# Padding the split tiles so that successive buffers lie at other offsets modulo 256 bytes

## The chip, the core and the metric

The kernel runs on one core of a Trainium2 chip. The metric is the device time of one execution in microseconds (us). Three runs of the kernel before took 2083.59, 2081.73 and 2076.95 us: a median of 2081.73.

## What is computed

One layer of an encoder trunk, applied with the same weights to a prompt of 512 tokens and to a sample of 2048 tokens, 1024 wide. One projection of the normed input gives everything else:

```python
h = rms_norm(x, pre_g)
z = h @ w_in
(q, k, v, gate_a, u_b, gate_b, c_val, c_glu, gate_c,
 merge_a, merge_b, merge_c) = jnp.split(z, split_pts, axis=-1)
y_a = neighbourhood_attention(heads(q), heads(k), heads(v), rpb) * jax.nn.silu(gate_a)
y_b = fourier_mix(u_b) * jax.nn.silu(gate_b)
y_c = conformer_conv(c_val, c_glu, dw_w, dw_b, cn_g, cn_b) * jax.nn.silu(gate_c)
merged = (jax.nn.sigmoid(merge_a) * (y_a @ w_a)
          + jax.nn.sigmoid(merge_b) * (y_b @ w_b)
          + jax.nn.sigmoid(merge_c) * (y_c @ w_c))
return x + rms_norm(merged @ w_o, post_g)
```

The attention looks at a window of 8 rows by 16 columns on a grid 64 wide, with 8 heads of 64; the Fourier mix is the real part of a 2-D transform; the convolution has 31 taps.

## The kernel before

**Split operands.** Every large matmul works on fp32 numbers that are held as two parts, high and low, in one tile `[128, 2, n]` of type fp32r. `split` (L133) writes the high part with a copy on ScalarE (L136) and the low part with a subtraction on VectorE (L137). A product is then three matmuls with 128 contracted rows: high by high, high by low, low by high. In `narrow` (L170 to L184) they are L180 to L182, with the weights stationary and 512 tokens (256 in the merge) moving:

```python
nc.tensor.matmul(ps, lhsT=u[:, 0, s], rhs=r[:, 0], start=n == 0, stop=False)
nc.tensor.matmul(ps, lhsT=u[:, 0, s], rhs=r[:, 1], start=False, stop=False)
nc.tensor.matmul(ps, lhsT=u[:, 1, s], rhs=r[:, 0], start=False, stop=n == len(kts) - 1)
```

Each of them is a weight load of 128 columns (the rows of PEld) and a matmul (the rows of PE). A block is eight steps of the contraction (kt), so 24 matmuls into one PSUM bank. In `wide` (L186, L194 to L196) tokens are stationary and 256 columns of weights move.

**Stages.** The tokens come as five chunks of 512: chunk 0 is the prompt, 1 to 4 the sample. Chunks 1 and 2, then 3 and 4, then 0 are projected: `proj_c`, `proj_qk`, `proj_v`, `proj_u`, `gates` and `merge_gates` take one weight unit after another from a list (`stream`, L158), and `emit_unit` (L139) loads a unit and splits it into two `w` tiles of a pool with five buffers. The tokens of a chunk are eight tiles `hT`, made by `make_h` (L219) or `raw_h` (L233) in two rings of 8 and 10 buffers (`ring`, `ring2`). Attention, convolution and Fourier transform are generators that `pump` (L283) advances between steps of the projections, so that their small matmuls (scores L603 and L604, transposes L636, `pv` L647, channel mean L480) stand among the projection's on TensorE. All activations go out to HBM. At the end, for each half chunk of 256 tokens, `prepare` (L805) loads and gates the branches into `ysp` tiles, `merge` (L828) multiplies by the resident weights `wb` through `narrow` and makes `msp` tiles, and `finish` (L855) multiplies by the resident `wo` in L869 to L871, with `msp` stationary and 512 columns of `wo` moving. `resident` (L1060) makes `wb` and `wo`.

**What sets the order.** The program's own order and a scheduler set each engine's order before the run; DMAs go through SP's queue.

**Where the tiles lie.** A `w` or `hT` tile takes 2 x 512 x 4 = 4096 bytes of each partition, a `wb` or `wo` tile 8192, an `ysp` or `msp` tile 4096. All are multiples of 256, and so is the distance between high and low part and between column slices of 128. So all buffers of a pool, and every slice that a matmul takes of one, share one offset modulo 256. In the allocation that is 32 for `w` and `hT`, 224 for `ysp` and `wb`, 128 for `wo` and `msp`; for the attention's tiles and the channel mean's `sp` it is 96, for the channel mean's stationary `ones` 0. Of a moving operand and the weights beside it the two offsets are equal, but for the channel mean, the transposes, part of the scores, and at the borders between stages. The first 16 KB of each partition are set aside as DMA scratch.

Of the kernel before, what the change touches and what calls it, by code (L numbers as in the profile page):

```python
# [16 lines left out]
F32R = mybir.dt.float32r  # L17
# [7 lines left out]
P = 128  # L25
D = 1024
KT = 8
C = 512
# [74 lines left out]
    return out.astype(np.float32)  # L103


class Build:
    def __init__(self, tc, a, out_p, out_s):
        self.tc, self.nc, self.a = tc, tc.nc, a
        self.outs = (out_p, out_s)
# [29 lines left out]
    def emit_unit(self, src, pieces=1):  # L139

        raw = self.wraw.tile([P, 1024], F32, tag="wraw", name="wraw")
        n = 1024 // pieces
        for i in range(0, 1024, n):
            self.load = self.nc.sync.dma_start(raw[:, i: i + n], src[:, i: i + n])
        ws = []
        for i in range(2):
            w = self.wsp.tile([P, 2, 512], F32R, tag="w", name="w")
            self.low = self.split(w, raw[:, i * 512: i * 512 + 512])
            ws.append(w)
        return ws  # L150
# [68 lines left out]
    def make_h(self, c, pool, tiles, ring):  # L219

        nc = self.nc
        rrow = pool.tile([P, C], F32, tag="rrow", name="rrow", bufs=1)
        nc.sync.dma_start(rrow, self.rs[c].to_broadcast([P, C]))
        for kt in range(KT):
            xr = pool.tile([P, C], F32, tag="xr", name="xr", bufs=3)
            nc.sync.dma_start(xr, self.a["xT"][kt * P: kt * P + P, c * C: c * C + C])
            nc.vector.scalar_tensor_tensor(xr, xr, self.preg[:, kt:kt + 1], rrow, op0=ALU.mult, op1=ALU.mult)
            t = ring.tile([P, 2, C], F32R, tag="h", name="hT")
            self.split(t, xr)
            tiles.append(t)  # L230
            yield

    def raw_h(self, c, tiles, ring):  # L233

        nc = self.nc
        for i in range(4):
            xr = self.ap.tile([P, 2, C], F32, tag="psp" if i % 2 else "vsp", name="xr", bufs=2)
            src = self.a["xT"][2 * i * P: 2 * i * P + 2 * P, c * C: c * C + C].rearrange("(k p) t -> p k t", p=P)
            apart = c == 1 and i == 0
            if not apart:  # L240
                nc.sync.dma_start(xr, src)
            for k in range(2):
                if apart:
                    nc.sync.dma_start(xr[:, k], src[:, k])
                g = self.preg[:, 2 * i + k: 2 * i + k + 1]
                t = ring.tile([P, 2, C], F32R, tag="h", name="hT")
                nc.scalar.mul(t[:, 0], xr[:, k], g)
                nc.vector.scalar_tensor_tensor(t[:, 1], xr[:, k], g, t[:, 0].bitcast(F32),  # L248
                                               op0=ALU.mult, op1=ALU.subtract)
                tiles.append(t)  # L250
                yield
# [553 lines left out]
    def prepare(self, c, hh, pool):  # L805

        nc = self.nc
        tok = slice(hh * 256, hh * 256 + 256)
        ysp = {}
        for b2 in (2, 3, 0, 1):  # L810
            if b2 < 2:
                y, low = (pool.tile([P, 2, 256], F32, tag="yl", name="yl", bufs=3) for _ in range(2))
                for i, t in enumerate((y, low)):
                    nc.sync.dma_start(t, self.ya[c][2 * b2: 2 * b2 + 2, i, :, tok].rearrange("b p t -> p b t"))
                nc.gpsimd.tensor_tensor(y, y, low, op=ALU.add)
            else:
                y = pool.tile([P, 2, 256], F32, tag="yl", name="yl", bufs=3)
                nc.sync.dma_start(y, self.yd[c][2 * b2 - 4: 2 * b2 - 2, :, tok].rearrange("b p t -> p b t"))
            g = pool.tile([P, 2, 256], F32, tag="gl", name="gl", bufs=2)
            nc.sync.dma_start(g, self.sg[c][2 * b2: 2 * b2 + 2, :, tok].rearrange("b p t -> p b t"))  # L820
            nc.vector.scalar_tensor_tensor(y, y, 0.5 if b2 == 3 else 1.0, g, op0=ALU.mult, op1=ALU.mult)  # L821
            t = pool.tile([P, 2, 2, 256], F32R, tag="ysp", name="ysp", bufs=5)
            self.split(t, y)
            for i in range(2):
                ysp[2 * b2 + i] = t[:, :, i]
        return ysp

    def merge(self, c, hh, ysp, pool, thp):  # L828

        nc = self.nc  # L830
        tok = slice(hh * 256, hh * 256 + 256)
        msp = {}
        for m2 in range(4):
            acc = pool.tile([P, 2, 256], F32, tag="acc", name="acc", bufs=2)
            for i in range(2):
                m = 2 * m2 + i
                th = thp.tile([P, 3, 256], F32, tag="th", name="th", bufs=3)
                nc.sync.dma_start(th, self.th[c][m][:, :, tok])
                pb = self.mm()
                for x, kts in enumerate(((4, 5), (6, 7))):  # L840
                    self.narrow(pb[:, x * 256: x * 256 + 256], self.wb[m], lambda kt: ysp[kt], kts)
                pa = self.mm()
                self.narrow(pa[:, :256], self.wb[m], lambda kt: ysp[kt], (0, 1, 2, 3))
                nc.vector.scalar_tensor_tensor(th[:, 1:3], th[:, 1:3], 1.0, pb.rearrange("p (x t) -> p x t", x=2),  # L844
                                               op0=ALU.add, op1=ALU.mult)
                nc.vector.scalar_tensor_tensor(acc[:, i], th[:, 0], 1.0, pa[:, :256], op0=ALU.add, op1=ALU.mult)
                nc.gpsimd.tensor_tensor(th[:, 1], th[:, 1], th[:, 2], op=ALU.add)
                nc.vector.tensor_tensor(acc[:, i], acc[:, i], th[:, 1], op=ALU.add)
            t = pool.tile([P, 2, 2, 256], F32R, tag="msp", name="msp", bufs=5)
            self.split(t, acc)  # L850
            for i in range(2):
                msp[2 * m2 + i] = t[:, :, i]
        return msp
# [42 lines left out]
    def run(self):  # L896
        tc, nc, a = self.tc, self.nc, self.a
        with ExitStack() as ctx:
# [36 lines left out]
            ring = F(tc.tile_pool(name="ring", bufs=8, side="left"))  # L935
# [11 lines left out]
            hT = {c: [] for c in range(NCH)}  # L947
# [96 lines left out]
            def prefetch():  # L1044
                while self.pos < base + 135:
                    yield
                att.close()
                pa = E(tc.tile_pool(name="pa", bufs=1, side="right", reuse_waits="tile"))
                state["pa"] = pa
                while self.pos < base + 163:  # L1050
                    yield
                fft.close()
                state["y"] = self.prepare(1, 0, pa)
                wbp = E(tc.tile_pool(name="wbp", bufs=1, side="right", reuse_waits="tile"))
                self.wb = []
                for _ in resident(a["wb"], wbp, self.wraw, "wraw", "wb", self.wb):
                    for _ in range(4):
                        yield

            def resident(src, pool, raw, tag, nm, out):  # L1060
                for i in range(KT):
                    r = raw.tile([P, 1024], F32, tag=tag, name="wraw", bufs=3 if tag == "wraw" else 2)
                    nc.sync.dma_start(r, src[i])
                    w = pool.tile([P, 2, 1024], F32R, tag=f"{nm}{i}", name=nm)
                    self.split(w, r)
                    out.append(w)
                    yield
# [10 lines left out]
            for _ in resident(a["wo"], mp, mp, "x", "wo", self.wo):  # L1078
                pass
            pa, ysp = state["pa"], state["y"]  # L1080
            order = [(c, hh) for c in (1, 2, 3, 4, 0) for hh in range(2)]
            for n, (c, hh) in enumerate(order):
                msp = self.merge(c, hh, ysp, mp, pa)
                if n + 1 < len(order):
                    ysp = self.prepare(*order[n + 1], pa)
# [51 lines left out]


def program(arrays):
    nc = bacc.Bacc("TRN2", target_bir_lowering=False, num_devices=1)  # L1140
    a = {k: nc.dram_tensor(k, v.shape, mybir.dt.from_np(v.dtype), kind="ExternalInput").ap()
         for k, v in arrays.items()}
    out_p = nc.dram_tensor("y_prompt", (1, 512, D), F32, kind="ExternalOutput").ap()
    out_s = nc.dram_tensor("y_sample", (1, 2048, D), F32, kind="ExternalOutput").ap()
    with tile.TileContext(nc, schedule_with_timeline_sim=True) as tc:  # L1145
        Build(tc, a, out_p, out_s).run()
    return nc
# [8 lines left out]
```

## Time and profile before

| | before |
|---|---|
| median of 3 runs | 2081.73 us (2076.95 to 2083.59) |
| the profiled execution's own time | 2078.99 us |
| its span, first to last instruction | 2077.2 us |
| TensorE busy | 2050.4 us, 99% of the span, 11184 matmuls |
| weight loads (PEld) | 1773.8 us, 85% |
| VectorE, ScalarE, GpSimd busy | 62%, 39%, 15% |
| TensorE clock granted, mean over the span | 0.997 |
| HBM read and written | 284.47 and 109.58 MB, 190 GB/s |

The profile is of one execution. Line numbers are those of the kernel before. Matmuls are pipelined: a row's duration reaches past the start of the next matmul, so the pace is read from starts in the timeline, which gives them to 0.01 us; over many rows the rounding goes away. PE stands for TensorE's matmuls, PEld for its weight loads, DVE for VectorE, ACT for ScalarE, POOL for GpSimd, SP for the queue of DMAs.

### The profile page before, as it was taken

How to read it: one execution, taken by the hardware profiler on the slowest of the kernel's cores; microseconds unless marked ns; L12 is line 12 of the kernel's file. 1: busy time of each engine (PE TensorE's matmuls, PEld its weight loads, DVE VectorE, ACT ScalarE, POOL GpSimd, SP SyncE). 2: the span in 40 equal slices, each digit the busy share in tenths (PEclk: the TensorE clock that was granted, in tenths of full speed). 3: DMA queues.
4: the chain of work that ended last, by engine and by line, in shares of the span. 5: the costliest groups of instructions: out<-in, count | busy, mean ns of one | idle time of the engine just before them, and what ended most of it. 6: DMA issues, size and time to landing. Idle time of an engine off the chain costs nothing. (4 is left out here: it accounts for less than half of the span.)

```text
span 2077.2 us, 31264 instructions
## 1 busy us (share of the span) xinstructions
PE 2050.4 (99%) x11184; PEld 1773.8 (85%) x11184; DVE 1296.3 (62%) x2853; ACT 801.3 (39%) x1649; POOL 301.6 (15%) x318
## 2 busy tenths in 40 slices
PE   8899999999999999999999999999999999999998
PEld 6779888888888899888888888898888989999997
DVE  6374557565454546776666655898854666666655
ACT  6422234343332224555555555336654211111111
POOL 0000011111100002322222221003200122222211
PEclk9999999999999999999999999999999999999999
DMA  9694544444443545666566676779897755555532
GB/s 328 202 250 159 181 140 147 142 149 146 142 153 117 152 132 174 178 177 198 172 172 182 177 221 187 239 252 271 267 325 252 225 177 176 185 169 183 178 131 79
DMA packets 241195, 388.79 MB, mean 187 GB/s; under 512 B 25376, under 2 KB 137632, under 8 KB 239136
## 3 DMA queue, kind: packets, MB, share of 16 engines
q1 hardware_dynamic: 241040, 386.80, 60.1%
q8 instruction: 88, 1.44, 0.3%
q14 instruction: 67, 0.55, 0.1%
HBM read 284.47 MB, written 109.58 MB: 190 GB/s over the span
## 5 line engine op out<-in xcount | busy, mean ns | idle before, releaser
L180 PE MATMUL mm<-hT,w 128*128 128x512 f32 x1760 | 699.6, 398 | 15.0 <-ACT w L136 7.1
L181 PE MATMUL mm<-hT,w 128*128 128x512 f32 x1760 | 691.2, 393 | 0.0
L182 PE MATMUL mm<-hT,w 128*128 128x512 f32 x1760 | 690.7, 393 | 0.0
L180 PEld LDWEIGHTS mm<-hT,w 128*128 128x128 f32 x1760 | 332.1, 189 | 79.2 <-ACT w L136 7.3
L182 PEld LDWEIGHTS mm<-hT,w 128*128 128x128 f32 x1760 | 331.7, 188 | 70.3 <-DVE w L137 0.8
L181 PEld LDWEIGHTS mm<-hT,w 128*128 128x128 f32 x1760 | 332.4, 189 | 62.6 <-DVE hT L248 1.0
L137 DVE TENSOR_TENSOR w<-wraw,w 128x512 fp32r<-128x512 f32 x308 | 220.4, 719 | 142.7 <-ACT w L136 138.0
L136 ACT CAST w<-wraw 128x512 fp32r<-128x512 f32 x308 | 189.0, 618 | 201.8 <-PE mm L182 166.2
L459 DVE SCALAR_TENSOR_TENSOR acc<-cb,cw,acc 128x512 f32<-128x512 f32 (+1 forms) x300 | 237.3, 793 | 2.9
L180 PE MATMUL mm<-ysp,wb 128*128 128x256 f32 x640 | 181.7, 284 | 3.8 <-DVE nw_y L118 3.8
L182 PE MATMUL mm<-ysp,wb 128*128 128x256 f32 x640 | 181.7, 284 | 0.0
L181 PE MATMUL mm<-ysp,wb 128*128 128x256 f32 x640 | 181.7, 284 | 0.0
L611 ACT ACTIVATE p<-p,m 128x384 f32<-128x384 f32 (+2 forms) x160 | 102.3, 639 | 153.0 <-DVE m L610 127.8
L607 DVE CUSTOM_DVE_ANT_0 p<-s,bias 128x384 f32<-128x384 f32 (+2 forms) x160 | 92.6, 580 | 104.7 <-PE pt L636 88.1
L574 POOL TENSOR_TENSOR bias<-tab,mask 128x384 f32<-128x384 f32 x64 | 67.4, 1056 | 572.1 <-DVE m L607 529.4
L566 POOL TENSOR_TENSOR bias<-tab,mask 128x512 f32<-128x512 f32 x64 | 85.9, 1344 | 367.5 <-DVE m L607 353.7
L195 PE MATMUL mm<-w,hT 128*128 128x256 f32 x480 | 135.5, 283 | 0.0
L196 PE MATMUL mm<-w,hT 128*128 128x256 f32 x480 | 135.5, 283 | 0.0
L194 PE MATMUL mm<-w,hT 128*128 128x256 f32 x480 | 135.2, 284 | 0.0
L180 PEld LDWEIGHTS mm<-ysp,wb 128*128 128x128 f32 x640 | 123.2, 193 | 5.4 <-DVE th L844 4.0
L870 PE MATMUL po<-wo,msp 128*128 128x512 f32 x320 | 124.5, 390 | 0.0
L869 PE MATMUL po<-wo,msp 128*128 128x512 f32 x320 | 124.3, 391 | 0.1
(154 smaller groups left out, 3000.0 us busy)
## 6 DMA issues: line engine op xcount, KB each, us to landing
wraw<-wn SPq DMA_DIRECT2D x135, 512.0 KB
th<-z SPq DMA_DIRECT2D x120, 256.0 KB
th<-th SPq DMA_DIRECT2D x80, 384.0 KB
qsp<-qd SPq DMA_DIRECT2D x80, 256.0 KB
tab<-tab SPq DMA_DIRECT2D x40, 384.0 KB
w<-dftd SPq DMA_DIRECT2D x14, 1024.0 KB
vsp<-vds SPq DMA_DIRECT2D x256, 48.0 KB
qd<-zs SPq DMA_DIRECT2D x20, 512.0 KB
```

Of the source, the lines that this page charges most:

```text
L136: nc.scalar.copy(dst[:, 0], src)
L137: return nc.vector.tensor_tensor(dst[:, 1], src, dst[:, 0].bitcast(F32), op=ALU.subtract)
L180: nc.tensor.matmul(ps, lhsT=u[:, 0, s], rhs=r[:, 0], start=n == 0, stop=False)
L181: nc.tensor.matmul(ps, lhsT=u[:, 0, s], rhs=r[:, 1], start=False, stop=False)
L182: nc.tensor.matmul(ps, lhsT=u[:, 1, s], rhs=r[:, 0], start=False, stop=n == len(kts) - 1)
L194: nc.tensor.matmul(ps, lhsT=r[:, 0, q], rhs=w[:, 0, s], start=kt == 0, stop=False)
L195: nc.tensor.matmul(ps, lhsT=r[:, 0, q], rhs=w[:, 1, s], start=False, stop=False)
L196: nc.tensor.matmul(ps, lhsT=r[:, 1, q], rhs=w[:, 0, s], start=False, stop=kt == KT - 1)
L459: nc.vector.scalar_tensor_tensor(acc[:, :n], cb[:, b, e:e + n], wv[:, e:e + 1], acc[:, :n], op0=ALU.mult, op1=ALU.add)
L611: nc.scalar.activation(p[:, :n], p[:, :n], AF.Exp, bias=m[:, 1:2], accum_out=m[:, 2:3])
L869: nc.tensor.matmul(po, lhsT=r[:, 0, q], rhs=w[:, 0], start=kt == 0, stop=False)
L870: nc.tensor.matmul(po, lhsT=r[:, 0, q], rhs=w[:, 1], start=False, stop=False)
```

## The change

A function `staggered` makes a tile with `pad` bytes behind each partition's row and returns the part without them. So the buffers of a pool follow each other at a distance of 4096 + 32 (`w`), 4096 + 160 (`hT`), 4096 + 32 (`ysp`), 4096 + 64 (`msp`), 8192 + 160 (`wb`) and 8192 + 32 bytes (`wo`). In the new allocation the five `w` buffers lie at 32, 64, 96, 128 and 160 modulo 256; the eight `hT` buffers of `ring` at eight different multiples of 32, the ten of `ring2` at the same eight, two of them (96 and 192) taken twice; the `wb` tiles and the `wo` tiles at eight different ones each; the five `ysp` at 64, 192, 160, 128 and 96, the five `msp` at 128, 192, 0, 64 and 128. Within a tile the high and low part and the slices keep one offset. The attention's tiles stay at 96. The padding takes room in the partition, and the scratch for DMAs is set to 2048 bytes in place of 16384.

Each engine's instructions stand in the same order as before and with the same buffers; a score of them, in the stretch where `wb` and `wo` are loaded, wait for other semaphores, since pools that take the place of earlier ones begin at other addresses.

```diff
+def staggered(pool, shape, pad, **kw):
+
+    n = math.prod(shape[1:])
+    t = pool.tile([P, n + pad // 4], F32R, **kw)[:, :n]
+    names = "abc"[:len(shape) - 1]
+    return t.rearrange(f"p ({' '.join(names)}) -> p {' '.join(names)}", **dict(zip(names, shape[1:])))
@@ emit_unit
-            w = self.wsp.tile([P, 2, 512], F32R, tag="w", name="w")
+            w = staggered(self.wsp, [P, 2, 512], 32, tag="w", name="w")
@@ make_h, and the same in raw_h
-            t = ring.tile([P, 2, C], F32R, tag="h", name="hT")
+            t = staggered(ring, [P, 2, C], 160, tag="h", name="hT")
@@ prepare
-            t = pool.tile([P, 2, 2, 256], F32R, tag="ysp", name="ysp", bufs=5)
+            t = staggered(pool, [P, 2, 2, 256], 32, tag="ysp", name="ysp", bufs=5)
@@ merge
-            t = pool.tile([P, 2, 2, 256], F32R, tag="msp", name="msp", bufs=5)
+            t = staggered(pool, [P, 2, 2, 256], 64, tag="msp", name="msp", bufs=5)
@@ resident
-                    w = pool.tile([P, 2, 1024], F32R, tag=f"{nm}{i}", name=nm)
+                    w = staggered(pool, [P, 2, 1024], 32 if nm == "wo" else 160, tag=f"{nm}{i}", name=nm)
@@ program
-    nc = bacc.Bacc("TRN2", target_bir_lowering=False, num_devices=1)
+    nc = bacc.Bacc("TRN2", target_bir_lowering=False, num_devices=1, dynamic_dma_scratch_size=2048)
```

## Rows read from the trace of the kernel before

**Rows 1.** The page: span, busy time, and TensorE's granted clock in 40 slices.
```profile
span 2077.2 us, 31264 instructions
PE 2050.4 (99%) x11184; PEld 1773.8 (85%) x11184; DVE 1296.3 (62%) x2853; ACT 801.3 (39%) x1649; POOL 301.6 (15%) x318
PEclk9999999999999999999999999999999999999999
```

**Rows 2.** Groups by line and form, whole run, one line of each three.
```profile
L180 PE MATMUL mm<-hT,w 128*128 128x512 f32 x1760 | 699.6, 398 | 15.0 <-ACT w L136 7.1 <-DVE z L319 6.6 <-DVE nw_t L128 1.3
...
L180 PE MATMUL mm<-ysp,wb 128*128 128x256 f32 x640 | 181.7, 284 | 3.8 <-DVE nw_y L118 3.8
...
L195 PE MATMUL mm<-w,hT 128*128 128x256 f32 x480 | 135.5, 283 | 0.0
...
L870 PE MATMUL po<-wo,msp 128*128 128x512 f32 x320 | 124.5, 390 | 0.0
```

**Rows 3.** Timeline of PE, undisturbed projections: start, duration in us; 43 rows, the ends.
```profile
664.89 0.39 PE L182 MATMUL mm<-hT,w 128*128 128x512 f32 x1
...
674.41 0.39 PE L182 MATMUL mm<-hT,w 128*128 128x512 f32 x1
```

**Rows 4.** Timeline of PE in the merge: the ends of 37 rows.
```profile
1853.42 0.28 PE L182 MATMUL mm<-ysp,wb 128*128 128x256 f32 x1
...
1857.74 0.28 PE L182 MATMUL mm<-ysp,wb 128*128 128x256 f32 x1
```

**Rows 5.** Windows: stretch, its us, busy us by engine, clock, DMA share, GB/s.
```profile
656.89:661.43 4.54, 4.54 (x22) 3.75 (x21) 0.69 (x1) 0.59 (x1) 0.00 (x0) 1.00 0.07 17
...
664.89:674.41 9.52, 9.52 (x44) 7.88 (x43) 2.87 (x5) 3.47 (x6) 1.04 (x1) 1.00 0.73 243
320.00:560.00 240.00, 240.00 (x1129) 199.32 (x1128) 143.09 (x316) 91.56 (x187) 26.59 (x24) 1.00 0.48 147
```

**Rows 6.** Timeline of PE around the channel mean's two matmuls (L480).
```profile
661.65 0.40 PE L182 MATMUL mm<-hT,w 128*128 128x512 f32 x1
661.89 0.62 PE L480 MATMUL cm<-sp,ones 128*128 128x512 f32 x2
662.34 0.40 PE L180 MATMUL mm<-hT,w 128*128 128x512 f32 x1
...
663.28 0.39 PE L181 MATMUL mm<-hT,w 128*128 128x512 f32 x1
663.50 0.39 PE L182 MATMUL mm<-hT,w 128*128 128x512 f32 x1
```

**Rows 7.** Timeline of PE: three pv matmuls among the projections.
```profile
305.16 0.51 PE L647 MATMUL pv<-psp,vsp 128*128 128x256 f32 x3
305.51 0.40 PE L180 MATMUL mm<-hT,w 128*128 128x512 f32 x1
```

**Rows 8.** Timeline of PE: merge behind an output matmul, the ends of 13 rows.
```profile
1865.24 0.28 PE L180 MATMUL mm<-ysp,wb 128*128 128x256 f32 x1
...
1866.66 0.28 PE L180 MATMUL mm<-ysp,wb 128*128 128x256 f32 x1
```

**Rows 9.** Groups of PE from 320 to 560 us.
```profile
L182 PE MATMUL mm<-hT,w 128*128 128x512 f32 x312 | 121.9, 391 | 0.0
L647 PE MATMUL pv<-psp,vsp 128*128 128x256 f32 x72 | 12.3, 280 | 0.0
L636 PE MATMUL pt<-ident,p 128*128 128x128 f32 x73 | 12.0, 271 | 0.0
L604 PE MATMUL s<-ksp,qsp 128*128 128x384 f32 x24 | 8.2, 342 | 0.0
```

**Rows 10.** The page: DMA queues, kind, packets, MB, share of 16 engines.
```profile
q1 hardware_dynamic: 241040, 386.80, 60.1%
q8 instruction: 88, 1.44, 0.3%
q14 instruction: 67, 0.55, 0.1%
```

More of the change, by code (lines that the diff above doesn't have):

```diff
@@ L245, in raw_h @@
                 g = self.preg[:, 2 * i + k: 2 * i + k + 1]
-                t = ring.tile([P, 2, C], F32R, tag="h", name="hT")
+                t = staggered(ring, [P, 2, C], 160, tag="h", name="hT")
                 nc.scalar.mul(t[:, 0], xr[:, k], g)
```

## The prediction

> **What bounds the kernel now.** I read the page first. TensorE is busy for 2050.4 of 2077.2 us, with the granted clock at the top digit in all 40 slices [rows 1]. The idle time ahead of L180, the first matmul of each step, is 15.0 us in the projections and 3.8 in the merge [rows 2]; so nothing that feeds PE decides, and the time is the number of matmuls times the distance from one matmul's start to the next. Busy time does not show that distance, since matmuls overlap; the timeline does.
>
> The groups by form give the counts [rows 2]: 3 x 1760 + 3 x 320 = 6240 matmuls of 512 columns (projections, L180 to L182, and output, L869 to L871), and 3 x 640 + 3 x 480 = 3360 of 256 columns (merge, and the wide projections, L194 to L196). Every one has a weight load of its own beside it. The attention's and the FFT's matmuls, some 1,600, use no padded buffer as an operand.
>
> Now the distances. In an undisturbed stretch 42 starts of 512 columns span 674.41 - 664.89 = 9.52 us, **0.2267 us** each [rows 3]. In the merge, 36 starts of 256 columns span 1857.74 - 1853.42 = 4.32 us, **0.120 us** each [rows 4]. [...]
>
> [...] The reader should compare the windows [rows 5]: the stretch from 656.89 to 661.43, with DMA at 7% and VectorE and ScalarE busy for about a seventh of it, holds 20 distances, 0.227 each; in the undisturbed stretch above DMA stands at 73%, VectorE at 30% and ScalarE at 36%, and the pace is the same. So I put nothing on writers. [...]
>
> Here the channel mean is a small experiment that the old kernel already contains. Its two matmuls read `sp` (96 modulo 256) against `ones` (0), between token matmuls whose operands both lie at 32. The length stays 512, yet from 661.65 three starts with unequal offsets span 662.34 - 661.65 = 0.69 us, 0.230 each, and then, with equal offsets again, the pace doesn't return at once: from 661.65 to 664.89 there are 14 distances in 3.24 us, **0.2314** each, before it is back at 0.2267 [rows 6, 3]. I call this unsettled. So equal offsets are not simply a bad case: a run with equal offsets settles, and a change of offsets throws it off for some ten matmuls.
>
> At 256 columns unsettled is the quicker one: three pv matmuls among tokens take 305.51 - 305.16 = 0.35 us, 0.117 each [rows 7], and twelve merge matmuls right behind an output matmul 1866.66 - 1865.24 = 1.42, 0.118 each [rows 8], against 0.120.
>
> **The change, part by part.** The order of instructions is the same on all five engines, and no instruction is added or removed. So the sum has three parts.
>
> *512 columns.* After the change the token offset moves by 160 bytes from one kt to the next, that is every third matmul, while the weight tile stays: the difference takes seven or eight multiples of 32 in a block. A run that needs some ten matmuls to settle would get three, so I expect the pace of the three unequal starts, 0.230, everywhere. What is it now? From 320 to 560, 240 us hold 1129 matmuls, 936 of them these [rows 5, 9]. The other 193 are 72 pv at 0.117, 73 transposes, which I take at 0.11 a little below pv's, and 48 scores, between pv's 0.117 and 0.227, taken at 0.18: 8.4 + 8.0 + 8.6 = 25 us. That leaves 215 / 936 = 0.2297. The mean of the whole run lies between this and the 0.2267 of stretches without attention; I take 0.2285 as an estimate, with 0.2267 and 0.2297 as its ends. Change: 0.0015 x 6240 = **+9.4 us**. Bounds: down to 0.22, the smallest distance in the unsettled run (663.28 to 663.50 [rows 6]), and up to 0.24, the largest; kept for a whole run neither is likely, and I take the mean of the three since it alone is with unequal offsets.
>
> *256 columns.* `ysp` against `wb` moves every sixth matmul, `w` against tokens every third. From 0.120 to between 0.117 and 0.118, say 0.0023 less: 0.0023 x 3360 = **-7.7 us**. Bounds: nothing, and 0.005 (twice what was seen) for -17 us.
>
> *The rest.* The smaller DMA scratch pays for the padding. The queue table has one data queue, hardware dynamic, with 386.80 MB, and two that carry instructions [rows 10]; no row shows a transfer that would need the scratch, and I cost it at nothing. The pools begin elsewhere, so some twenty instructions in the prefetch (casts of `wb` and `wo`, two loads on SP's queue, a sum on GpSimd) wait for other semaphores than before; behind them on SP stand `yl` and `gl` loads. They run a stage ahead of PE, which waits for 3.8 us in the merge [rows 2]; under the matmuls of the last merge gates they cost nothing, and if that cover went, another wait of that size, 4 us.
>
> Sum: +9.4 - 7.7 = +1.7 us on the profiled execution's 2078.99 us (span 2077.2), so 2080.7; the median of the runs shown is 2081.73, 0.13% above it. I round to **2080**.
>
> [...]
>
> **The rivals.**
>
> [...]
>
> [...]
>
> *Loss: PE never settles and 256 columns gain nothing.* The place is the 512-column blocks of gates and merge gates. With the whole unsettled run's 0.2314 there, +0.0029 x 6240 = +18 us, 2097. It decides from where the new mean passes 0.2285 + 6.2 / 6240 = 0.2295 with nothing won at 256 columns, or 0.2307 with the 7.7 us. For it: the 14 distances [rows 6]. Against it: most of these were with equal offsets.
>
> *Nothing at all.* Offsets don't matter and the channel mean disturbs PE by its wait or its PSUM bank. Then 2079. Against it: the first matmul of each projection block also waits and changes bank, and the undisturbed stretch, which crosses such borders, shows nothing of it [rows 3].
>
> **How the numbers follow.** Within 0.3%, about what a measurement of this kernel can tell from no change, is 6.2 us. Near-cancelling (my forecast) 0.38, with its own range 2068 to 2092, of which 0.05 lies beyond on the quick side and 0.06 on the slow side; settling lower 0.27; all of it gone 0.07; loss 0.22; nothing 0.06. So faster 0.05 + 0.27 + 0.07 = 0.39, slower 0.22 + 0.06 = 0.28, same 0.27 + 0.06 = 0.33. The range, 2045 to 2100, reaches from the gain case at almost its full size to the loss at 2097 with a little over; it leaves out the 1940 case and the far ends of gain and loss, some 2 in 10 together.
>
> **What would show it.** Right: in the stretch of merge gates that was at 0.2267 throughout, starts now vary from row to row with a mean near 0.230, and the merge's 36 starts span about 4.23 us where they spanned 4.32. Wrong to the quick side: 24 starts of a projection block in under 5.4 us. Wrong to the slow side: over 5.54 us. If the block reads 5.44 with every row alike, offsets did nothing. PE waits of more than 5 us in the prefetch of `wb` and `wo` would mean that the moved pools, which I cost at nothing, matter.

## The result, and the profile after

| | before | after |
|---|---|---|
| median of 4 runs each | 2080.85 us | 2092.23 us (2090.57 to 2098.76) |
| ratio, 95% interval | | 1.0062 [1.0035, 1.0089] |
| span of the profiled execution | 2077.2 us | 2091.0 us |

I forecast 2080 us; the change makes the kernel slower by 0.6%: 11 us in the medians, 13.8 us between the two profiled spans. Lines of the kernel after are eight higher: L188 to L190 are the old L180 to L182, L202 to L204 the wide ones, L877 to L879 the output, L488 the channel mean.

The page of after, which answers to [rows 1]:
```profile
span 2091.0 us, 31268 instructions
PE 2065.7 (99%) x11184; PEld 1769.3 (85%) x11184; DVE 1295.4 (62%) x2853; ACT 802.7 (38%) x1649; POOL 302.5 (14%) x318
PEclk9999999999999999999999999999999999999999
```
The same number of matmuls, the same clock (0.997 in the mean of either span), VectorE, ScalarE and GpSimd as busy as before to within 2 us: it is PE's busy time that grew, by 15.3 us. The page counts four instructions more than before, where the prediction had none added; in the programs these are four more waits on semaphores, none of them on PE. The groups by form, against [rows 2]:
```profile
L188 PE MATMUL mm<-hT,w 128*128 128x512 f32 x1760 | 703.5, 400 | 15.1 <-ACT w L144 7.2 <-DVE z L327 6.9 <-ACT hT L255 1.0
L188 PE MATMUL mm<-ysp,wb 128*128 128x256 f32 x640 | 180.3, 282 | 2.2 <-DVE nw_y L126 2.2
L203 PE MATMUL mm<-w,hT 128*128 128x256 f32 x480 | 134.6, 281 | 0.0
L878 PE MATMUL po<-wo,msp 128*128 128x512 f32 x320 | 126.0, 394 | 0.0
```
Idle time ahead of L188 is 15.1 us in the projections (15.0 before) and 2.2 in the merge (3.8 before): no wait came in. The mean duration of a 512-column matmul went up by 2 to 4 ns and that of a 256-column matmul down by 2, so the two kinds moved in opposite ways. Durations overlap, so the sizes come from the starts. In the timeline of PE after (start and duration in us) the first rows are the stretch around the channel mean and the merge gates behind it, as in [rows 6, 3], then the merge of [rows 4]:
```profile
669.40 0.39 PE L190 MATMUL mm<-hT,w 128*128 128x512 f32 x1
...
672.65 0.39 PE L190 MATMUL mm<-hT,w 128*128 128x512 f32 x1
...
678.21 0.39 PE L190 MATMUL mm<-hT,w 128*128 128x512 f32 x1
...
682.35 0.39 PE L190 MATMUL mm<-hT,w 128*128 128x512 f32 x1
...
1866.57 0.28 PE L190 MATMUL mm<-ysp,wb 128*128 128x256 f32 x1
...
1870.85 0.28 PE L190 MATMUL mm<-ysp,wb 128*128 128x256 f32 x1
```
The 42 distances that spanned 9.52 us now span 682.35 - 672.65 = 9.70, 0.2310 each; 24 starts take 678.21 - 672.65 = 5.56 us. The 14 distances across the channel mean take 3.25 us, where they took 3.24: what was the exception before is now the rule. The merge's 36 distances take 4.28 us in place of 4.32.

Adding up every start-to-start distance of a trace by the kind of matmul that begins it shows where the 13.8 us are:

| kind | count | mean distance before, us | after | sum of distances, waits included |
|---|---|---|---|---|
| projections, 512 columns | 5280 | 0.2290 | 0.2322 | +16.4 us |
| output, 512 columns | 960 | 0.2277 | 0.2320 | +3.8 us |
| merge, 256 columns | 1920 | 0.1198 | 0.1181 | -4.9 us (1.6 of it a shorter wait) |
| wide, 256 columns | 1440 | 0.1199 | 0.1184 | -2.2 us |
| all others | 1584 | 0.1272 | 0.1275 | +0.6 us |

The means of the first four rows leave out distances over 0.3 us (0.15 us at 256 columns), which hold waits; the last row's mean holds all. Such means are what "pace" stands for below.

### The profile page after: what moved, and what is told of

The parts are those of the page before. It is cut to its first block, busy times and chain, and to the rows that moved or that the text cites. A ratio compares the mean times of both kernels' runs of the same rounds, so it can differ in the third digit from the quotient of the medians.

```text
span 2091.0 us, 31268 instructions
## 1 busy us (share of the span) xinstructions
PE 2065.7 (99%) x11184; PEld 1769.3 (85%) x11184; DVE 1295.4 (62%) x2853; ACT 802.7 (38%) x1649; POOL 302.5 (14%) x318
## 5 line engine op out<-in xcount | busy, mean ns | idle before, releaser
L188 PE MATMUL mm<-hT,w 128*128 128x512 f32 x1760 | 703.5, 400 | 15.1 <-ACT w L144 7.2
L190 PE MATMUL mm<-hT,w 128*128 128x512 f32 x1760 | 696.6, 396 | 0.1
L188 PEld LDWEIGHTS mm<-hT,w 128*128 128x128 f32 x1760 | 332.5, 189 | 84.9 <-ACT w L144 7.4
L190 PEld LDWEIGHTS mm<-hT,w 128*128 128x128 f32 x1760 | 332.0, 189 | 74.0 <-DVE w L145 0.7
L188 PE MATMUL mm<-ysp,wb 128*128 128x256 f32 x640 | 180.3, 282 | 2.2 <-DVE nw_y L126 2.2
L190 PE MATMUL mm<-ysp,wb 128*128 128x256 f32 x640 | 180.2, 282 | 0.0
L204 PE MATMUL mm<-w,hT 128*128 128x256 f32 x480 | 134.4, 281 | 0.0
L202 PE MATMUL mm<-w,hT 128*128 128x256 f32 x480 | 134.2, 282 | 0.0
L877 PE MATMUL po<-wo,msp 128*128 128x512 f32 x320 | 125.4, 394 | 0.0
L188 PEld LDWEIGHTS mm<-ysp,wb 128*128 128x128 f32 x640 | 121.2, 189 | 3.9 <-DVE th L852 2.4
```

Of the source, the lines that this page charges most:

```text
L202: nc.tensor.matmul(ps, lhsT=r[:, 0, q], rhs=w[:, 0, s], start=kt == 0, stop=False)
L204: nc.tensor.matmul(ps, lhsT=r[:, 1, q], rhs=w[:, 0, s], start=False, stop=kt == KT - 1)
L877: nc.tensor.matmul(po, lhsT=r[:, 0, q], rhs=w[:, 0], start=kt == 0, stop=False)
```

## The experiments

Four theories were open. A: changing the difference of the two offsets throws PE off, and any constant difference settles. B: an unequal difference costs by itself, each value its own, and the stagger gives their average. C: some constant difference is quicker than 0. D: part of the loss comes from the DMA scratch or the moved pools.

**Constant differences.** Every tile is padded by 256 bytes, so that a pool has one offset again, and the slice begins `off` bytes further on. Difference means moving minus stationary operand, modulo 256. The scratch stays at 2 KB.

```diff
-def staggered(pool, shape, pad, **kw):
+def staggered(pool, shape, off, **kw):
-    t = pool.tile([P, n + pad // 4], F32R, **kw)[:, :n]
+    t = pool.tile([P, n + 64], F32R, **kw)[:, off // 4: off // 4 + n]
```

With `off` 32 for `ring`, 64 for `ring2`, 32 for `ysp` and `wo`, 0 elsewhere (d32_64):

```diff
-t = staggered(ring, [P, 2, C], 160, tag="h", name="hT")
+t = staggered(ring, [P, 2, C], 64 if ring.name == "ring2" else 32, tag="h", name="hT")
-t = staggered(pool, [P, 2, 2, 256], 64, tag="msp", name="msp", bufs=5)
+t = staggered(pool, [P, 2, 2, 256], 0, tag="msp", name="msp", bufs=5)
-w = staggered(pool, [P, 2, 1024], 32 if nm == "wo" else 160, tag=f"{nm}{i}", name=nm)
+w = staggered(pool, [P, 2, 1024], 32 if nm == "wo" else 0, tag=f"{nm}{i}", name=nm)
@@ w: 32 becomes 0; ysp stays at 32, wb gets 0
```

> Buffers stay 256 bytes apart, so each pool keeps one offset, but the offsets of the two operands differ by a constant: tokens 32 (ring) or 64 bytes (ring2) from the weights, ysp 32 from wb, wo 32 from msp. Theory A, changes unsettle: a constant difference settles like equal offsets, 24 distances of a projection block without attention in 5.44 us (0.2267 each), merge at 0.120, time 2076 to 2085 us. Theory B, unequal costs: 0.230 or more throughout at 512 columns, 0.1175 at 256, time 2085 to 2097. Theory C, some differences are better: a settled pace below 0.2267 in one of the blocks, time below 2075.

The same four places with 96, 128, 64 and 64 (d96_128):

> The same with other constants: tokens 96 (ring) or 128 bytes (ring2) from the weights, ysp 64 from wb, wo 64 from msp. A: 0.2267 and 0.120 once settled, 2076 to 2085 us. B: 0.230 or more and 0.1175, 2085 to 2097. C: a settled pace below 0.2267 or 0.120 in one of them, below 2075.

With 160, 192, 96 and 96 (d160_192):

> The same: tokens 160 (ring) or 192 bytes (ring2) from the weights, ysp 96 from wb, wo 96 from msp. A: 0.2267 and 0.120 once settled, 2076 to 2085 us. B: 0.230 or more and 0.1175, 2085 to 2097. C: a settled pace below 0.2267 or 0.120 in one of them, below 2075.

With 224, 0, 128 and 128 (d224_0):

> The same: tokens 224 (ring) or 0 bytes (ring2, so chunks 1 and 3 are as before) from the weights, ysp 128 from wb, wo 128 from msp. A: 0.2267 and 0.120 once settled, 2076 to 2085 us. B: 0.230 or more and 0.1175 except in chunks 1 and 3, 2082 to 2092. C: a settled pace below 0.2267 or 0.120 in one of them, below 2075.

| run | median, us | ratio to before |
|---|---|---|
| d32_64 | 2091.69 | 1.0051 [1.0035, 1.0067] |
| d96_128 | 2096.80 | 1.0059 [1.0027, 1.0092] |
| d160_192 | 2107.91 | 1.0113 [1.0082, 1.0145] |
| d224_0 | 2092.76 | 1.0049 [1.0032, 1.0065] |

The ratios are followed by their 95% intervals. None is quicker than before, and none is at its time, though no difference changes within a block; d160_192, from two runs, lies above the 2085 to 2097 of theory B as well. Timeline of PE of d32_64: pairs of starts that are 60 matmuls apart, at difference 64 (tokens of `ring2`), 32 (tokens of `ring`), and 32 in the merge:
```profile
18.02 0.40 PE L188 MATMUL mm<-hT,w 128*128 128x512 f32 x1
...
31.76 0.40 PE L188 MATMUL mm<-hT,w 128*128 128x512 f32 x1
...
1580.99 0.40 PE L189 MATMUL mm<-hT,w 128*128 128x512 f32 x1
...
1594.99 0.40 PE L189 MATMUL mm<-hT,w 128*128 128x512 f32 x1
...
1722.79 0.28 PE L188 MATMUL mm<-ysp,wb 128*128 128x256 f32 x1
...
1729.86 0.28 PE L188 MATMUL mm<-ysp,wb 128*128 128x256 f32 x1
```
At 64 the 60 distances take 13.74 us, 0.2290 each; at 32 they take 14.00, **0.2333**, over a stretch without any change of offset. The merge's take 7.07, 0.1178: this stretch and the one behind it are slow ones, the other long stretches of that merge have 0.1167. The same places of d224_0, where they are at difference 0 and at 224, and wide matmuls at 32:
```profile
17.78 0.39 PE L188 MATMUL mm<-hT,w 128*128 128x512 f32 x1
...
31.38 0.39 PE L188 MATMUL mm<-hT,w 128*128 128x512 f32 x1
...
169.26 0.28 PE L202 MATMUL mm<-w,hT 128*128 128x256 f32 x1
...
176.26 0.28 PE L202 MATMUL mm<-w,hT 128*128 128x256 f32 x1
...
1581.57 0.40 PE L189 MATMUL mm<-hT,w 128*128 128x512 f32 x1
...
1595.56 0.40 PE L189 MATMUL mm<-hT,w 128*128 128x512 f32 x1
```
Difference 0 gives 13.60 us, 0.2267, the old pace; 224 gives 13.99. At 256 columns it is the other way round: 7.00 us for 60, 0.1167, against 0.1200 at difference 0.

Mean pace in us once a difference has lasted for at least 14 matmuls, over the four runs and, for 0, the kernel before:

| difference | 0 | 32 | 64 | 96 | 128 | 160 | 192 | 224 |
|---|---|---|---|---|---|---|---|---|
| 512 columns | 0.2267 | 0.2333 | 0.2290 | 0.2333 | 0.2326 | 0.2342 | 0.2333 | 0.2333 |
| merge | 0.1200 | 0.1168 | 0.1178 | 0.1200 | 0.1186 | | | |
| wide | 0.1200 | 0.1167 | 0.1163 | 0.1199 | 0.1193 | 0.1178 | 0.1164 | 0.1183 |

The output gave 0.2333, 0.2289, 0.2334 and 0.2324 at 32 to 128, at other places in memory than the projections: among multiples of 32 the difference decides at 512 columns, to within half a nanosecond. At 256 columns merge and wide matmuls differ by up to 1.5 ns at one difference, and some of these means are of two paces (more on that below). The mean of the row for 512 columns is 0.2320, and after has 0.2320 to 0.2322; the wide row's mean is 0.1181, and after has 0.1184. So theory B holds for what lasts and for the average: an unequal difference that never changes has a pace of its own. A falls, since most constant differences cost as much as one that changes; C falls at 512 columns and holds at 256, where 32 and 64 are quickest.

**All offsets back, scratch and pools as after.** `off` is 0 everywhere:

```diff
-    w = staggered(self.wsp, [P, 2, 512], 32, tag="w", name="w")
+    w = staggered(self.wsp, [P, 2, 512], 0, tag="w", name="w")
@@ and so for hT, ysp, msp, wb, wo
```

> Every padded tile back at the offset that it had before (pads of 256 bytes, so all of a pool share one offset), but the 2 KB of DMA scratch and the moved pools stay. Theory B (the cost is the unequal offset of moving and stationary operand by itself): no change against the kernel before, 2081 us within 0.3%, the mean distance of the projections' 512-column matmuls 0.229, of the merge 0.120. Rival D (part of the change's 11 us comes from the scratch or from the waits that the moved pools changed): 2084 us or more with the same distances and longer waits of PE around the loading of the resident weights.

Measured: 2081.27 us, ratio 0.9996 [0.9982, 1.0010]; pace 0.2290 and 0.1198, as before. From the groups of this run:
```profile
L188 PE MATMUL mm<-hT,w 128*128 128x512 f32 x1760 | 700.0, 398 | 16.3 <-ACT w L144 7.3 <-DVE z L327 6.7 <-DVE nw_t L136 1.5
```
The idle time is 16.3 us (15.0 before). D falls: scratch and moved pools cost nothing that can be measured, as I had put it.

**The change in two halves.** Only `w` and `hT` padded as in the change, the others with a pad of 0 (tokens_alone):

```diff
-t = staggered(pool, [P, 2, 2, 256], 32, tag="ysp", name="ysp", bufs=5)
+t = staggered(pool, [P, 2, 2, 256], 0, tag="ysp", name="ysp", bufs=5)
-t = staggered(pool, [P, 2, 2, 256], 64, tag="msp", name="msp", bufs=5)
+t = staggered(pool, [P, 2, 2, 256], 0, tag="msp", name="msp", bufs=5)
-w = staggered(pool, [P, 2, 1024], 32 if nm == "wo" else 160, tag=f"{nm}{i}", name=nm)
+w = staggered(pool, [P, 2, 1024], 0, tag=f"{nm}{i}", name=nm)
```

> Only the w and hT tiles are padded as in the change, with the 2 KB of scratch; ysp, wb, msp and wo have no padding and equal offsets again. Theory B (each of the eight differences costs its own pace, parts add up): the 5280 projection matmuls go from 0.2290 to 0.2321, +16.4 us, the wide ones from 0.1199 to 0.1184, -2.2 us, merge and output as before: +14 us, about 2096, ratio 1.007, so slower than the whole change. Rival F (the loss comes from the output matmuls and the end of the program, since the stretch of the projections has other work to hide it): 2080 to 2084.

Measured: 2094.47 us, ratio 1.0063 [1.0044, 1.0081]; projections at 0.2322, wide at 0.1184, merge and output as before. Sorted by the offsets that the allocation gives each matmul, the projections' means at differences 0, 32, 64 and so on to 224 are 0.2316, 0.2319, 0.2315, 0.2337, 0.2324, 0.2332, 0.2311 and 0.2322. In visits of three matmuls the eight lie closer together than in the table: 0 and 64 are slower, 32, 160, 192 and 224 quicker. So the stagger doesn't simply string the lasting paces together, and why the two averages agree is not shown. And the reverse, a pad of 0 for `w` and `hT` only (merge_output_alone):

> Only ysp, msp, wb and wo are padded as in the change, with the 2 KB of scratch; w and hT have no padding. Theory B: merge 1920 x (0.1181 - 0.1198) = -3.3 to -4.9 us, output 960 x (0.2320 - 0.2277) = +3.8 to +4.1 us, together -1 to +1: about 2081, ratio 1.000. Rival F: 2090 or more, the loss of the whole change.

Measured: 2082.18 us, ratio 1.0004 [0.9988, 1.0019]; output at 0.2320, merge at 0.1181. The parts add up within what the runs can tell: the loss lies in the projections, and merge and output cancel each other. F, a loss at the output and the end, falls.

**Taking only the gain.** All as in all_equal, but `ysp` at `off` 32 (merge_32):

```diff
-t = staggered(pool, [P, 2, 2, 256], 0, tag="ysp", name="ysp", bufs=5)
+t = staggered(pool, [P, 2, 2, 256], 32, tag="ysp", name="ysp", bufs=5)
```

> As all_equal, but the ysp tiles lie 32 bytes behind the wb tiles modulo 256. Theory B with the table of the constant differences: the merge's 1920 matmuls go from 0.1200 to 0.1168, 3.2 ns each, -6.1 us, so about 2075 and a ratio of 0.997; nothing else moves. Rival E (the distance is only handed back at the next wait, since what feeds the merge, the loads and the split of ysp, follows at its own pace): merge starts at 0.1168 but PE's waits there grow by as much, and the time stays at 2081.

Measured: **2075.15 us**, ratio 0.9969 [0.9957, 0.9981]. Timeline of PE in its merge, 60 distances at difference 32:
```profile
1717.68 0.28 PE L188 MATMUL mm<-ysp,wb 128*128 128x256 f32 x1
...
1724.68 0.28 PE L188 MATMUL mm<-ysp,wb 128*128 128x256 f32 x1
```
7.00 us, 0.1167 each. Then also 64 for the `w` tiles of the wide units (merge_32_wide_64):

```diff
-wide = [w[g, i] for g in range(3) for i in range(2)]
+self.wides = wide = [w[g, i] for g in range(3) for i in range(2)]
-w = staggered(self.wsp, [P, 2, 512], 0, tag="w", name="w")
+w = staggered(self.wsp, [P, 2, 512], 64 * any(src is u for u in self.wides), tag="w", name="w")
```

> As merge_32, and the w tiles of the wide units alone lie 64 bytes behind the others, so the wide matmuls have a difference of 64. Theory B: another 3.6 ns for each of 1440 matmuls, -5.2 us, about 2070 and a ratio of 0.9945 to the kernel before. Rival E: PE waits for other things instead and the time is that of merge_32, 2075.

Measured: **2069.86 us**, ratio 0.9937 [0.9915, 0.9960]; wide at 0.1170, projections at 0.2290 as before. E, that the matmuls' gain is handed back at the next wait, falls in both. This version beats the kernel before and the change.

The 0.1170 is a mean of two paces. Timeline of PE of this run, wide matmuls, starts that are 60 apart, in two stretches with the same offsets modulo 256 and so the same difference of 64:
```profile
745.44 0.28 PE L202 MATMUL mm<-w,hT 128*128 128x256 f32 x1
...
752.51 0.28 PE L202 MATMUL mm<-w,hT 128*128 128x256 f32 x1
...
769.51 0.28 PE L202 MATMUL mm<-w,hT 128*128 128x256 f32 x1
...
776.31 0.28 PE L202 MATMUL mm<-w,hT 128*128 128x256 f32 x1
```
The first take 7.07 us, 0.1178 each, the second 6.80, **0.1133**. Each pace holds for a whole stretch of some 180 to 200 matmuls, up to the next matmul of the attention. So the offsets modulo 256 alone don't always fix the pace; what picks one of the two no run asked. At difference 0 on a multiple of 32, long stretches of projections, merge and wide matmuls agree within 0.2 ns over all these traces.

**Finer than 32 bytes.** `off` 16 for `ring`, 8 for `ring2`, 16 for `ysp` and `wo` (d16_8):

```diff
-t = staggered(ring, [P, 2, C], 0, tag="h", name="hT")
+t = staggered(ring, [P, 2, C], 8 if ring.name == "ring2" else 16, tag="h", name="hT")
@@ ysp 16, wo 16, all others 0
```

> Constant differences finer than 32: 16 for the tokens of one ring, 8 for those of the other, 16 in merge and output. If what counts is a bank or word of 32 bytes or more, the pace is that of difference 0: 0.2267 at 512 columns, 0.120 at 256, and about 2081 us. If every unequal byte address counts alike, 0.233 and 0.117 as at a difference of 32, and about 2098.

Measured, one run: 2100.57 us. Timeline of PE: 8 at 512 columns, 248 in the wide matmuls, where the tokens are stationary, and 16 at 512 columns:
```profile
17.43 0.40 PE L188 MATMUL mm<-hT,w 128*128 128x512 f32 x1
...
31.43 0.40 PE L188 MATMUL mm<-hT,w 128*128 128x512 f32 x1
...
165.26 0.28 PE L202 MATMUL mm<-w,hT 128*128 128x256 f32 x1
...
172.19 0.28 PE L202 MATMUL mm<-w,hT 128*128 128x256 f32 x1
...
1591.27 0.40 PE L189 MATMUL mm<-hT,w 128*128 128x512 f32 x1
...
1605.16 0.40 PE L189 MATMUL mm<-hT,w 128*128 128x512 f32 x1
```
0.2333 at 8 and 0.2315 at 16: small differences don't count as 0. And 0.1155 for the wide ones, below every mean of the table at 256 columns (single stretches at 64 and 192 had 0.1133). I took that to be a matter of the difference 248, and put it on merge and wide matmuls by moving the moving tile 8 bytes back: `off` 248 for `ysp` and for the wide units' `w` (diff_248_at_256).

```diff
-t = staggered(pool, [P, 2, 2, 256], 32, tag="ysp", name="ysp", bufs=5)
+t = staggered(pool, [P, 2, 2, 256], 248, tag="ysp", name="ysp", bufs=5)
-w = staggered(self.wsp, [P, 2, 512], 64 * any(src is u for u in self.wides), tag="w", name="w")
+w = staggered(self.wsp, [P, 2, 512], 248 * any(src is u for u in self.wides), tag="w", name="w")
```

> All at the old equal offsets but for the 256-column matmuls, whose moving tiles (ysp, and the w tiles of the wide units) lie 8 bytes before the stationary ones modulo 256. Theory B with the 0.1156 that the wide matmuls of d16_8 showed at this difference: merge 1920 x 4.2 ns = -8.1 us, wide 1440 x 4.3 ns = -6.2 us, so about 2067, ratio 0.993, and 3 us below merge_32_wide_64. If the sign of the difference doesn't carry from wide to merge: the merge is at 0.1168 to 0.1184, and the time 2069 to 2073.

Measured: 2080.37 us, ratio 1.0000 [0.9985, 1.0016]: a miss. Timeline of PE, wide matmuls:
```profile
158.47 0.28 PE L202 MATMUL mm<-w,hT 128*128 128x256 f32 x1
...
165.67 0.28 PE L202 MATMUL mm<-w,hT 128*128 128x256 f32 x1
```
7.20 us for 60, 0.1200, at the same difference at which d16_8 had 0.1155. In d16_8 the moving tile lay at 32 modulo 256 and the stationary one at 40; here they lie at 24 and 32. Beside it ran `off` 248 for `ring`, 4 for `ring2` and `ysp`, 8 for `wo` (d248_4_8):

```diff
-t = staggered(ring, [P, 2, C], 0, tag="h", name="hT")
+t = staggered(ring, [P, 2, C], 4 if ring.name == "ring2" else 248, tag="h", name="hT")
@@ ysp 4, wo 8, all others 0
```

> Finer differences at 512 columns: 248 for the tokens of one ring, 4 for those of the other, 8 in the output; 4 in the merge, 8 and 252 in the wide matmuls. Theory B in the form that only difference 0 has the settled pace: 0.229 to 0.234 in all three, about 2095 to 2100. Rival G (the pace depends on a word of 8 or 16 bytes, so that 4 counts as 0): 0.2267 at difference 4 for 512 columns and 0.120 in the merge, about 2088 to 2093. A pace below 0.2267 at any of them would be a gain that the change missed.

Measured, one run: 2119.31 us, the slowest of all. Timeline of PE at difference 4, 512 columns and merge:
```profile
15.90 0.40 PE L188 MATMUL mm<-hT,w 128*128 128x512 f32 x1
...
30.20 0.40 PE L188 MATMUL mm<-hT,w 128*128 128x512 f32 x1
...
1743.00 0.29 PE L188 MATMUL mm<-ysp,wb 128*128 128x256 f32 x1
...
1750.40 0.29 PE L188 MATMUL mm<-ysp,wb 128*128 128x256 f32 x1
```
0.2383 and 0.1233: worse than any multiple of 32 for both kinds, and so the time lies above the 2095 to 2100 of theory B. G, by which 4 counts as 0, falls. So below 32 bytes something else counts beside the difference, and two runs asked whether it is the place of the moving operand. First, both operands 8 bytes further on, difference 0 (both_8):

```diff
-t = staggered(ring, [P, 2, C], 0, tag="h", name="hT")
+t = staggered(ring, [P, 2, C], 8, tag="h", name="hT")
-w = staggered(self.wsp, [P, 2, 512], 0, tag="w", name="w")
+w = staggered(self.wsp, [P, 2, 512], 8, tag="w", name="w")
@@ ysp 8, wb 8
```

> Moving and stationary tiles of projections, wide matmuls and merge all 8 bytes further than before: difference 0, but no tile starts at a multiple of 32 any more; the output as before. H1 (the difference alone decides, and diff_248_at_256 failed for another reason): 0.2267 and 0.120 as before, about 2081. H2 (a moving operand that starts off a multiple of 32 costs by itself): 0.230 or more at 512 columns, 0.120 or more at 256, about 2095 to 2105. A third way: the distance has the settled value and 256 columns change alone.

Measured, one run: 2105.88 us. Timeline of PE, 512 columns:
```profile
1597.36 0.39 PE L189 MATMUL mm<-hT,w 128*128 128x512 f32 x1
...
1611.30 0.39 PE L189 MATMUL mm<-hT,w 128*128 128x512 f32 x1
```
13.94 us for 60, 0.2323, where the same difference had 0.2267; the 256 columns stayed at 0.1200, and the output, not moved, at 0.2275. That is what H2 forecast, that a moving operand off a multiple of 32 costs by itself; but the stationary operand left its multiple too, so which of the two costs it isn't separated. Second, merge_32_wide_64 with the stationary side moved in the merge: `off` 0 for `ysp` and 8 for `wb` (stationary_8):

```diff
-t = staggered(pool, [P, 2, 2, 256], 32, tag="ysp", name="ysp", bufs=5)
+t = staggered(pool, [P, 2, 2, 256], 0, tag="ysp", name="ysp", bufs=5)
-w = staggered(pool, [P, 2, 1024], 0, tag=f"{nm}{i}", name=nm)
+w = staggered(pool, [P, 2, 1024], 0 if nm == "wo" else 8, tag=f"{nm}{i}", name=nm)
```

> As merge_32_wide_64, but in the merge the moving ysp tiles stay at their old place, a multiple of 32, and the stationary wb tiles lie 8 bytes further (difference 248, as in the wide matmuls of d16_8, where the moving tile was at a multiple of 32 too). H2: 0.1156 in the merge, 1.1 ns below merge_32, so about 2068, ratio 0.9930, the quickest version so far. H1 (difference 248 as in diff_248_at_256): 0.120 in the merge and 2076.

Measured: 2071.47 us, ratio 0.9940 [0.9919, 0.9960]. Timeline of PE in the merge:
```profile
1709.20 0.28 PE L188 MATMUL mm<-ysp,wb 128*128 128x256 f32 x1
...
1716.13 0.28 PE L188 MATMUL mm<-ysp,wb 128*128 128x256 f32 x1
```
6.93 us for 60, 0.1155, as in d16_8 and not the 0.1200 of diff_248_at_256. So H1, that the difference alone decides, falls: at the difference 248 every long stretch of the merge is at 0.1155 to 0.1157 in stationary_8, with the moving tile on a multiple of 32 and the stationary one 8 bytes past one, and at 0.1200 in diff_248_at_256, with the moving tile 8 bytes before one and the stationary one on it. And the stationary tile 8 bytes on is not enough, since both_8 had it too and 0.1200. H2 fits, but the two operands moved together between these runs, and that the moving one's place decides is not shown. The 2 us that this should have brought against merge_32_wide_64 don't show in the median; its runs lie between 2064.13 and 2074.44, so the two can't be told apart.

## Why the prediction was wrong

The forecast of 2080 came from two terms that nearly cancel, +9.4 and -7.7. The measured ones are +21 and -5.5, and they don't.

**What bounds the kernel** was right. PE is the bound before and after, the waits moved it by less than 2 us, and the pace of the two kinds of matmul is what changed.

**The rest, at nothing,** was right: all_equal is at 0.9996 with the scratch and the moved pools of the change.

**The term of the 256 columns** had the right sign and was a little too large. Predicted: 0.0023 us less for 3360 matmuls, -7.7. Measured: 0.0017 less for the 1920 of the merge and 0.0015 for the 1440 wide ones, -3.3 - 2.2 = -5.5, and another 1.6 us from waits that were shorter in this trace.

**The term of the 512 columns** is the step that failed. Predicted: from 0.2285 to "the pace of the three unequal starts, 0.230, everywhere", +9.4. Measured: from 0.2288 (projections and output together) to 0.2321, 0.0033 x 6240 = +21. The old mean was estimated well; the new one was not, for two reasons.

The first is how the row was read. The 0.230 came from three distances that span 0.69 us, and they are not three unequal starts: the first, from 661.65 to 661.89, begins at a token matmul with equal offsets, and the two that begin at the channel mean's matmuls span 662.34 - 661.89 = 0.45 us, 0.225 each. Two or three distances behind a change are too few for a pace. The offsets there differ by 96, and d96_128 shows 0.2333 wherever that difference lasts. The other value that stood in [rows 6], the 14 distances at 0.2314, was the better measured one, and I used it only for the rival.

The second is the reason given: that an equal pair "settles" and a change throws it off. Half of it holds. After a disturbance, difference 0 does take some ten matmuls to come back: in the trace before, the means by place in an undisturbed run of projection matmuls fall from 0.2316 at the second to 0.2291 at the tenth and 0.2267 at the thirteenth. In the stagger it has some three: tokens_alone shows 0.2316 at 0 and 0.2315 at 64, where lasting runs have 0.2267 and 0.2290. But the other six need no change to be slow; they have 0.2326 to 0.2342 when nothing changes. The average comes out nearly the same either way, 0.2320 and 0.2322. So the slow pace is not only a passing state that the stagger prolongs; of the places tried, equal offsets on a multiple of 32 are the best for 512 columns, and the change leaves them. Why equal offsets are quicker there stays open.

**The rivals.** The loss, put at 2097 with 0.2314, was nearest to 2092: it had the 512 columns right within a nanosecond and missed the gain at 256. That it came so near is partly luck, since most of the 14 distances behind its 0.2314 were with equal offsets, as the prediction itself says. Its own point of decision, a new mean of 0.2307 with the gain at 256 columns kept, was passed. The 0.27 on settling lower, which gives the range its lower end of 2045, and the 0.07 on all of it gone, the 1940 case, count on 13.3 ns on top of every matmul of either length. No run shows such a term. What the runs show at 512 columns, at all eight multiples of 32 and at 4, 8, 16 and 248, is no lasting pace under 0.2267, and at 256 columns none under 0.1155 but for a few stretches at 0.1133. "Nothing at all" falls with tokens_alone and merge_32, whose intervals leave out 1.

**What would show it.** The signs were named rightly: 24 starts in over 5.54 us (they take 5.56) was the mark of the slow side. The merge's 36 distances take 4.28 us, between the 4.32 of before and the 4.23 expected; that stretch is not the best one, and the mean over all of the merge, 0.1181, would make 4.25.

## What to carry to other kernels

In this kernel, where PE is busy for 99% of the span and the idle time ahead of the first matmul of each step is 15.0 us in the projections and 3.8 in the merge, the place of the two operands in the partition was worth a few per cent of each matmul, and the sign depended on the length: of the places tried, 512 columns did best with both operands at the same offset modulo 256 and on a multiple of 32 (0.2267 us, against 0.2290 to 0.2383), and 256 columns gained about 7 and 5 us in the medians from operands 32 apart (merge) and 64 apart (wide). So one rule for all buffers was wrong here, and another kernel has to be measured; set the offset per pair of pools, by the kind of matmul that reads them (here that gave -0.6% where the stagger of everything gave +0.6%). And a pace that a prediction rests on is to be read over tens of starts, never over three, and with each distance put down to the matmul that begins it.

## What the runs showed of the hardware

None of this was expected, and why it is so stays open: the runs moved addresses and nothing else, and did not vary the weight load, the data type or the partitions.

- With a weight load beside every matmul, in fp32r and at a granted clock of 0.995 to 0.998 in the mean of each profiled execution, the mean distance over lasting stretches goes from 0.2267 to 0.2383 us at 512 columns and from 0.1155 to 0.1233 at 256 (0.1133 in single stretches), in runs that differ in the places of the two operands. The pace depends on both places together: in the merge, moving only the moving tiles by 32 bytes took it from 0.1200 to 0.1168, moving only the weights by 8 took it to 0.1155, and moving both by 8 left it at 0.1200. What causes this no run shows.
- One pair of offsets modulo 256 can have two lasting paces: in merge_32_wide_64 the wide matmuls ran at 0.1178 in one stretch and at 0.1133 in another, with the same offsets, in one execution whose mean granted clock was 0.996.
- With both operands 8 bytes past a multiple of 32, 512 columns are slower even at equal offsets: 0.2323 where 0.2267 was had. Which of the two costs it was not separated. The two starts 8 bytes off cost 6 ns of 227.
- Difference 4 is the worst place that was tried, at both lengths (0.2383 and 0.1233).
